# Query and key heads transposed in pairs, with wider gMLP output products and re-spaced spatial products, in a sparse-attention decoder layer

## The chip, the cores and the metric

The kernel runs on one core of a Trainium2 chip. The metric is the time of one execution on the device in microseconds (us). The profile that is read here is that of one further execution of the same program.

## What is computed

One layer of a decoder over a prompt of 2048 positions (16 blocks of 128) and a sample of 64 new positions (8 sequences by 8). All products are of float32 accuracy.

```python
h = rmsnorm(x, norm_g)
z = h @ w_in                       # 1024 -> 3656 columns
q, k, v, qi, ki, wi, ga, u, vm, gm = split(z)
q, k   = rope(rmsnorm(q)), rope(rmsnorm(k))     # 8 query heads, 4 key heads, 64 wide
qi, ki = rope(qi), rope(ki)                     # indexer: 8 heads x 64, one key of 64
score  = sum_h wi[h] * relu(qi[h] @ ki.T)       # causal
mask   = the 256 highest scores of each query
o      = softmax(q @ k.T / 8 over mask) @ v * silu(ga)
vn     = layernorm(gelu(vm))
s      = tril(w_s[group]) @ vn (in chunks of 128 positions) + b_s
gm_out = gelu(u) * s * silu(gm)
r      = x + concat(o, gm_out) @ w_out
y      = r + sigmoid(rmsnorm(r) @ w_ple_gate) * (p @ w_ple_proj)
```

Keys, values, indexer keys and the sample's `vn` are outputs as well. The sample attends to 1024 paged past positions of its own sequence and to the new ones.

## The kernel before

Float32 accuracy comes from splitting an operand into a rounded high part and the remaining low part (`split`, lines 121 to 124: ScalarE copies the high part out of PSUM, VectorE subtracts it for the low part) and adding high by high, high by low and low by high products.

**Phase A** (`phase_a`) goes through the blocks in three rounds (line 55; block 16, called SB, is the sample), and in each round through 14 column chunks of `w_in` (line 57), 256 columns wide except the first, x1, of 328. For each chunk `load_w` brings the weights: in round 0 as eight raw pieces, which GpSimd (line 288) and VectorE (line 289) scale and split, and `keep_w` stores the halves to DRAM; in later rounds the stored halves are loaded. `raw` has six buffers, each weight half two. `proj` makes a chunk's product for a block (24 matmuls), `post` works on it. `spatial` multiplies one of eight groups of `vn` for all blocks of a round at once; it is called while the chunk named k is under way, spread over its blocks.

Beside this, `pump` deals out pieces of the indexer's work after each product: `idx` computes a block's scores (line 683 and 684 for each head and 512 keys; ScalarE takes the relu at line 686, VectorE adds at line 688), `topk` finds the 256th score. A block is primed (its loads are issued) when the one ahead of it starts. The indexer's keys lie in SBUF with the high part in partitions 0 to 63 and the low part in 64 to 127, so a query head has to be present in both halves of the partitions. `load_qi` gets that by loading each head twice side by side, and each of the 8 heads is transposed by itself (line 668).

When the last chunk is done, `gm_product` multiplies the gMLP output by its half of `w_out` (lines 574, 575 and 578), in two halves of 256 columns of a 512-wide result, while the last top-k ends and `prep_early` prepares the attention: `twice` copies each key head next to itself, `prep_kv` transposes 4 heads (line 1016), `prep_q` 8 query heads that were loaded twice (lines 994 and 1031).

**Phase B** (`phase_b`) goes through steps of block and key head: scores (lines 1098 to 1100), exponentials (line 1107), transposed probabilities (line 1133), values (line 1150). The next block's queries are prepared at the third of a block's four steps. **Phase C** does the rest of the output projection, the gate and the result.

The tile framework lays out every engine's order at build time, by a simulation with estimated costs, and waits on semaphores keep the data right. An engine then works through its order as laid out; an instruction whose operand is late holds up all that stand behind it on its engine. DMAs are issued from SP's queue, in order, except gathers, which GpSimd issues.

## Time and profile before

| | |
|---|---|
| median of 3 runs (lowest to highest) | 1905.88 us (1904.62 to 1906.0) |
| profiled execution | 1905.45 us |
| its span, first to last instruction | 1903.7 us |
| TensorE busy in the span | 1845.6 us, 97% |
| VectorE, ScalarE, GpSimd busy | 65%, 54%, 33% |
| mean granted TensorE clock | 0.99 |

PE is TensorE's matmul stream, PEld its weight loads, DVE VectorE, ACT ScalarE, POOL GpSimd, SP the queue that issues most DMAs. Matmuls overlap: one takes longer from start to end than the next one starts behind it, so the distance between starts is what a matmul costs in a dense stream. A busy time counts the union of the spans.

### The profile page before, as it was taken

Reading aid. Unit: us, or ns where it says so; the run is one execution under the profiler, and the core shown is the slowest. Engines: PE = TensorE matmul, PEld = TensorE weight load, DVE = VectorE, ACT = ScalarE, POOL = GpSimd, SP = SyncE. Lnnn points to the kernel's source line nnn. Section 1 sums busy time; section 2 is a strip of 40 time slices with the busy share of each in tenths; the row PEclk is TensorE's granted clock in tenths of the full one; section 3 lists DMA queues with packets and bytes.
Section 4 is the critical chain, followed back from the end, with each engine's and each line's share of the span. In section 5 each row is a group of like instructions: output and inputs, shape, how many; then the busy total and the mean of one; then the engine's idle time right before and its main releaser. Section 6 shows DMA issues by size and latency. Waiting matters only on the chain. (4 is left out here: it accounts for less than half of the span.)

```text
span 1903.7 us, 34773 instructions
## 1 busy us (share of the span) xinstructions
PE 1845.6 (97%) x12374; PEld 1627.9 (86%) x12374; DVE 1244.3 (65%) x3623; ACT 1018.5 (54%) x1909; POOL 629.3 (33%) x950
## 2 busy tenths in 40 slices
PE   7989999999999999999999899999999989999998
PEld 6989979998999999999999777778777767888887
DVE  4597655478778638779852789879898854223321
ACT  4244435246556536676664888768787743222221
POOL 4583463332003224014303543232223164222211
PEclk9989999999999999999999999999999999999999
DMA  8645655644444554454554543232222073222211
GB/s 288 209 157 185 232 177 201 196 130 126 150 149 162 203 181 135 142 184 156 156 183 138 140 115 92 59 109 71 74 59 73 25 252 137 80 96 95 102 36 45
DMA packets 180578, 261.59 MB, mean 137 GB/s; under 512 B 83176, under 2 KB 129968, under 8 KB 176688
## 3 DMA queue, kind: packets, MB, share of 16 engines
q1 hardware_dynamic: 174512, 240.45, 38.8%
q0 software_dynamic: 5888, 18.88, 3.3%
q8 instruction: 98, 1.61, 0.4%
q14 instruction: 80, 0.66, 0.1%
HBM read 171.90 MB, written 87.37 MB: 136 GB/s over the span
## 5 line engine op out<-in xcount | busy, mean ns | idle before, releaser
L319 PE MATMUL z<-whi,hhi 128*128 128x256 f32 (+1 forms) x1792 | 463.2, 292 | 10.7 <-DVE qn L379 2.5
L320 PE MATMUL z<-wlo,hhi 128*128 128x256 f32 (+1 forms) x1792 | 456.9, 288 | 0.2 <-DVE wlo L289 0.2
L319 PEld LDWEIGHTS z<-whi,hhi 128*128 128x128 f32 x1792 | 344.8, 192 | 22.2 <-ACT kin L358 3.2
L320 PEld LDWEIGHTS z<-wlo,hhi 128*128 128x128 f32 x1792 | 345.1, 193 | 5.3 <-DVE wlo L289 1.5
L322 PE MATMUL z<-whi,hlo 128*128 128x256 f32 (+1 forms) x1792 | 270.2, 288 | 0.0
L322 PEld LDWEIGHTS z<-whi,hlo 128*128 128x128 f32 x1792 | 241.8, 192 | 4.0
L688 DVE SCALAR_TENSOR_TENSOR big<-dots,sgn,big 128x1024 f32<-128x1024 f32 (+7 forms) x176 | 179.2, 1018 | 61.0 <-ACT dots L686 59.5
L686 ACT ACTIVATE dots<-dots 128x1024 f32<-128x1024 f32 (+7 forms) x176 | 140.9, 803 | 108.2 <-PE dots L684 104.8
L124 DVE TENSOR_TENSOR b_pt<-b_tp,b_pt 128x512 fp32r<-128x512 f32 (+1 forms) x288 | 183.3, 655 | 11.3 <-ACT b_pt L123 9.8
L1150 PE MATMUL b_o<-b_pt,Vst 128*128 128x512 f32 x544 | 185.0, 425 | 0.6 <-DVE b_pt L124 0.4
L123 ACT ACTIVATE b_pt<-b_tp 128x512 fp32r<-128x512 f32 (+1 forms) x288 | 156.0, 578 | 47.2 <-PE b_tp L1133 37.9
L1133 PE MATMUL b_tp<-mats,b_sm 128*128 128x128 f32 x1088 | 171.8, 276 | 3.8 <-ACT b_sm L1107 2.8
L1107 ACT ACTIVATE b_sm<-b_sm,b_st 128x128 f32<-128x128 f32 (+15 forms) x128 | 154.6, 1209 | 19.5 <-DVE b_st L1100 18.4
L1133 PEld LDWEIGHTS b_tp<-mats,b_sm 128*128 128x128 f32 x1088 | 133.7, 142 | 34.1 <-ACT b_sm L1107 7.3
L824 ACT ACTIVATE bfw<-big,tk 128x384 bf16<-128x384 f32 (+14 forms) x105 | 136.4, 1299 | 48.1 <-DVE tk L844 30.0
L1098 PE MATMUL b_s<-Kst,b_qh 128*128 128x512 f32 (+3 forms) x320 | 140.8, 441 | 7.7 <-DVE b_st L1100 4.5
L1100 DVE CUSTOM_DVE_ANT_0 b_sm<-b_s,b_mask,b_st 128x512 f32<-128x512 f32 (+3 forms) x192 | 123.9, 645 | 27.9 <-PE b_s L1099 23.2
L1099 PE MATMUL b_s<-Kst,b_ql 128*128 128x512 f32 (+3 forms) x320 | 117.4, 369 | 0.0
L683 PE MATMUL dots<-ki_stack,qih 128*128 128x512 f32 (+3 forms) x304 | 113.0, 374 | 1.4 <-DVE big L688 1.4
L684 PE MATMUL dots<-ki_stack,qil 128*128 128x512 f32 (+3 forms) x304 | 110.2, 372 | 0.0
L1150 PEld LDWEIGHTS b_o<-b_pt,Vst 128*128 128x128 f32 x544 | 90.3, 190 | 23.2 <-DVE b_pt L124 6.6
L1460 PE MATMUL c_mm<-c_h_w_ple_gate,c_mh 128*128 128x512 f32 x272 | 109.0, 401 | 0.2 <-ACT c_mh L123 0.2
(350 smaller groups left out, 3871.6 us busy)
## 6 DMA issues: line engine op xcount, KB each, us to landing
whi<-s_wh SPq DMA_DIRECT2D x52, 512.0 KB
wlo<-s_wl SPq DMA_DIRECT2D x52, 512.0 KB
raw<-w_in SPq DMA_DIRECT2D x112, 128.0 KB
s_wh<-whi SPq DMA_DIRECT2D x13, 1024.0 KB
s_wl<-wlo SPq DMA_DIRECT2D x13, 1024.0 KB
s_r<-hlo SPq DMA_DIRECT2D x32, 256.0 KB
b_qr<-s_q SPq DMA_DIRECT2D x32, 256.0 KB
c_r<-s_r SPq DMA_DIRECT2D x16, 512.0 KB
```

The source lines that it names most:

```text
L123: nc.scalar.activation(hi, src, AF.Copy)
L124: nc.vector.tensor_tensor(lo, src, hi.bitcast(F32), OP.subtract)
L319: nc.tensor.matmul(z, lhsT=hh[:, k], rhs=wh[:, k, :n], start=(k == 0), stop=False)
L320: nc.tensor.matmul(z, lhsT=hh[:, k], rhs=wl[:, k, :n], start=False, stop=False)
L322: nc.tensor.matmul(z, lhsT=hl[:, k], rhs=wh[:, k, :n], start=False, stop=(k == 7))
L686: nc.scalar.activation(r, r, AF.Relu)
L688: nc.vector.scalar_tensor_tensor(a, r, self.sgn[:, b, h:h + 1], a, op0=OP.mult, op1=OP.add)
L824: nc.scalar.activation(junk, acc[:P], AF.Sign, bias=cur[:, 0:1], accum_out=cur[:, 1:2])
L1098: nc.tensor.matmul(ps, lhsT=qh[:, h], rhs=rhs, start=True, stop=False)
L1107: nc.scalar.activation(part, part, AF.Exp, bias=stt[:, h, c:c + 1], scale=-1.0, accum_out=stt[:, h, 4 + e:5 + e])
L1133: nc.tensor.transpose(ps[:, k, r], sm2[r][:, (k0 + k) * 128:(k0 + k) * 128 + 128], ident)
L1150: nc.tensor.matmul(o.rearrange("p a b -> p (a b)"), lhsT=Vst[:, kb, g].rearrange("p a d -> p (a d)"), rhs=pt[:, k].rearrange("p a b -> p ( ...
```

## The change

- The two halves of the weights of a chunk are kept with 328 elements from one row of eight to the next in every chunk, not with as many as the chunk is wide. `raw` has four buffers, not six.
- `gm_product` makes one product of 512 columns where it made two of 256; `load_out` places the weights for that.
- The spatial products are spread over the chunks k (from its third block on) and v.
- In round 2 the blocks are scored from 15 down to 11.
- Two heads lie side by side in a load and are transposed together. A new function, `heads`, splits the transposed pair: each head's high and low part are written to the partitions on which it lies, and get to the other half of the partitions by four DMAs within SBUF, or, for attention blocks 0 to 4 (`direct`), by further instructions of ScalarE and VectorE. `idx` does this when a block is primed. `prep_q` is called at a block's first step instead of its third, with the load of the block after. Keys are transposed in pairs as well and written to both halves by ScalarE and VectorE; `twice` goes. The indexer's key is no longer doubled ahead of its transpose, and block SB's is not transposed.
- The iota that seeds a block's scores is made anew for each block on GpSimd (`order`), and the stored one goes. The sample's indexer takes its buffers from the new tiles (not shown).

```diff
-DUE = ROUNDS
+DUE = ROUNDS[:2] + [ROUNDS[2][::-1]]
...
-        rp = pool("a_raw", 6)
+        rp = pool("a_raw", 4)
...
-            return [wp.tile([128, 8 * 328], F32R, name=f"w{e}")[:, :8 * n].rearrange("p (k n) -> p k n", k=8)
-                    for e in ("hi", "lo")]
+            return [wp.tile([128, 8, 328], F32R, name=f"w{e}")[:, :, :n] for e in ("hi", "lo")]
...
-            wh, wl = halves(256)
+            wh, wl = (t.rearrange("p k n -> p (k n)")[:, :2048].rearrange("p (k n) -> p k n", k=4) for t in halves(328))
             for i in range(8):
                 raw = rp.tile([128, 328], F32, name="raw")[:, :256]
-                k, c0 = 4 + i % 4, j * 512 + i // 4 * 256
-                nc.sync.dma_start(raw, I["w_out"][0, k * 128:(k + 1) * 128, c0:c0 + 256])
-                nc.gpsimd.tensor_scalar(wh[:, i], raw, 1.0, 1.0, op0=OP.mult, op1=OP.mult)
-                nc.gpsimd.tensor_tensor(wl[:, i], raw, wh[:, i].bitcast(F32), OP.subtract)
+                k, c0 = i // 2, i % 2 * 256
+                nc.sync.dma_start(raw, I["w_out"][0, 512 + k * 128:640 + k * 128, j * 512 + c0:j * 512 + c0 + 256])
+                nc.gpsimd.tensor_scalar(wh[:, k, c0:c0 + 256], raw, 1.0, 1.0, op0=OP.mult, op1=OP.mult)
+                nc.gpsimd.tensor_tensor(wl[:, k, c0:c0 + 256], raw, wh[:, k, c0:c0 + 256].bitcast(F32), OP.subtract)
...
-                kin2 = wk.tile([128, 2, 64], F32, name="kin")[:P]
-                nc.scalar.activation(kin2, z[:, None, 0:64].to_broadcast([P, 2, 64]), AF.Copy, scale=rs)
-                self.rope(nc.vector, kin2, rt, 2, wk, P)
-                kin = kin2[:, 0]
+                kin = wk.tile([128, 64], F32, name="kin")[:P]
+                nc.scalar.activation(kin, z[:, 0:64], AF.Copy, scale=rs)
+                self.rope(nc.vector, kin[:, None, :], rt, 1, wk, P)
                 dst = O["idx_k_sample"].rearrange("o a t d -> (o a t) d") if b == SB else O["idx_k_prompt"][0, 0, b * 128:(b + 1) * 128]
                 nc.sync.dma_start(dst, kin)
 
                 def ki_t():
                     ps = self.tp.tile([128, 4, 128], F32, name="tp")
-                    nc.tensor.transpose(ps[:, 0, :P], kin2.rearrange("p a d -> p (a d)"), ident[:P, :P])
-                    kst = self.ki[:, b, :P]
-                    nc.scalar.activation(kst, ps[:, 0, :P], AF.Copy)
-                    nc.vector.tensor_tensor(kst[64:128], ps[64:128, 0, :P], kst[64:128].bitcast(F32), OP.subtract)
-
-                later.append(ki_t)
+                    nc.tensor.transpose(ps[:64, 0], kin, ident)
+                    kst = self.ki[:, b]
+                    nc.scalar.activation(kst[0:64], ps[:64, 0], AF.Copy)
+                    nc.vector.tensor_tensor(kst[64:128], ps[:64, 0], kst[0:64].bitcast(F32), OP.subtract)
+
+                if b != SB:
+                    later.append(ki_t)
...
-                iota = ac.tile([128, SEQ], mybir.dt.int16, name="iota")
-                nc.gpsimd.iota(iota, pattern=[[1, SEQ]], base=0, channel_multiplier=0)
-                self.iota = iota
...
-                if name == "k":
-                    for g in range(8 * j // len(blocks), 8 * (j + 1) // len(blocks)):
+                n, s = 2 * len(blocks) - 2, {"k": j - 2, "v": len(blocks) - 2 + j}.get(name, -1)
+                if s >= 0:
+                    for g in range(8 * s // n, 8 * (s + 1) // n):
                         spatial(blocks, g)
...
-            for i in range(2):
-                z = zt[:, i * 256:i * 256 + 256]
+            for k in range(4):
+                nc.tensor.matmul(zt, lhsT=hh[:, k], rhs=wh[:, k], start=(k == 0), stop=False)
+                nc.tensor.matmul(zt, lhsT=hh[:, k], rhs=wl[:, k], start=False, stop=(b == SB and k == 3))
+            if b != SB:
                 for k in range(4):
-                    nc.tensor.matmul(z, lhsT=hh[:, k], rhs=wh[:, i * 4 + k, :256], start=(k == 0), stop=False)
-                    nc.tensor.matmul(z, lhsT=hh[:, k], rhs=wl[:, i * 4 + k, :256], start=False, stop=(b == SB and k == 3))
-                if b != SB:
-                    for k in range(4):
-                        nc.tensor.matmul(z, lhsT=hh[:, 4 + k], rhs=wh[:, i * 4 + k, :256], start=False, stop=(k == 3))
+                    nc.tensor.matmul(zt, lhsT=hh[:, 4 + k], rhs=wh[:, k], start=False, stop=(k == 3))
...
+def order(self, acc, P):
+    nc = self.nc
+    nc.gpsimd.iota(acc[:P], pattern=[[1, acc.shape[1]]], base=0, channel_multiplier=0,
+                   allow_small_or_imprecise_dtypes=True)
+    nc.gpsimd.tensor_scalar(acc[:P], acc[:P], -UNIT, 1.0, op0=OP.mult, op1=OP.mult)
+
+def heads(self, pool, names, ps, bufs, direct=False):
+    nc = self.nc
+    qh, ql = (pool.tile([128, 2, 4, 128], F32R, name=n, bufs=bufs) for n in names)
+    own = [slice(0, 64), slice(64, 128)]
+    for e in range(2):
+        nc.scalar.activation(qh[own[e], e], ps[own[e]], AF.Copy)
+        nc.vector.tensor_tensor(ql[own[e], e], ps[own[e]], qh[own[e], e].bitcast(F32), OP.subtract)
+        if direct:
+            nc.scalar.activation(qh[own[1 - e], e], ps[own[e]], AF.Copy)
+            nc.vector.tensor_tensor(ql[own[1 - e], e], ps[own[e]], qh[own[e], e].bitcast(F32), OP.subtract)
+    if direct:
+        return qh, ql
+    for t in (qh, ql):
+        for e in range(2):
+            nc.sync.dma_start(t[own[1 - e], e].bitcast(F32), t[own[e], e].bitcast(F32))
+    return qh, ql
+
 def idx(self, b):
     nc, wk, wk2 = self.nc, self.wk, self.wk2
     W = 128 * (b + 1)
-    qds = self.load_qi(b)
+    qd = wk2.tile([128, 4, 128], F32, name="qid", bufs=2)
+    nc.sync.dma_start(qd, self.s_qi[b].rearrange("p (h d) -> p h d", h=4))
+    ps = self.tp.tile([128, 4, 128], F32, name="tp")
+    for j in range(4):
+        nc.tensor.transpose(ps[:, j], qd[:, j], self.ident)
+    qh, ql = self.heads(wk2, ("qih", "qil"), ps, 2)
     yield None
-    qh, ql = [], []
-    for j in range(2):
-        qd = qds[j].rearrange("p h a d -> p h (a d)")
-        ps = self.tp.tile([128, 4, 128], F32, name="tp")
-        for h in range(4):
-            nc.tensor.transpose(ps[:, h], qd[:, h], self.ident)
-        qh.append(wk2.tile([128, 4, 128], F32R, name="qih", bufs=3))
-        ql.append(wk2.tile([128, 4, 128], F32R, name="qil", bufs=3))
-        self.split(qh[j], ql[j], ps)
-        yield 2
     acc = self.big.tile([128, SEQ], F32, name="big")[:, :W]
-    nc.gpsimd.tensor_scalar(acc, self.iota[:, :W], -UNIT, 1.0, op0=OP.mult, op1=OP.mult)
+    self.order(acc, 128)
...
-                nc.tensor.matmul(ps[:, s0:s0 + sn], lhsT=qh[h // 4][:, h % 4], rhs=rhs, start=True, stop=False)
-                nc.tensor.matmul(ps[:, s0:s0 + sn], lhsT=ql[h // 4][:, h % 4], rhs=rhs, start=False, stop=True)
+                nc.tensor.matmul(ps[:, s0:s0 + sn], lhsT=qh[:, h % 2, h // 2], rhs=rhs, start=True, stop=False)
+                nc.tensor.matmul(ps[:, s0:s0 + sn], lhsT=ql[:, h % 2, h // 2], rhs=rhs, start=False, stop=True)
...
-        q = io.tile([128, 8, 2, 64], F32, name="b_qr", bufs=1)
+        q = io.tile([128, 4, 128], F32, name="b_qr", bufs=1)
         ga = io.tile([128, 512], F32, name="b_ga")
-        for a in range(2):
-            nc.sync.dma_start(q[:, :, a], self.s_q[i].rearrange("t (h d) -> t h d", h=8))
+        nc.sync.dma_start(q, self.s_q[i].rearrange("t (h d) -> t h d", h=4))
...
-    def twice(i):
-        kds[i] = raw.tile([128, 4, 2, 64], F32, name="b_kd")
-        nc.scalar.copy(kds[i], kvs[i][0].rearrange("p (h d) -> p h d", h=4)[:, :, None, :].to_broadcast([128, 4, 2, 64]))
...
-        k, v = kds.pop(i), kvs.pop(i)[1]
+        k, v = kvs.pop(i)
         ps = psum()
-        for g in range(4):
-            nc.tensor.transpose(ps[:, g], k[:, g].rearrange("p a d -> p (a d)"), ident)
-        ks = Kst[i // 4][:, :, (i % 4) * 128:(i % 4) * 128 + 128]
-        nc.scalar.activation(ks, ps, AF.Copy)
-        V.tensor_tensor(ks[64:128], ps[64:128], ks[64:128].bitcast(F32), OP.subtract)
+        for j in range(2):
+            nc.tensor.transpose(ps[:, j], k[:, j * 128:j * 128 + 128], ident)
+        ks = Kst[i // 4].rearrange("p (j e) n -> p j e n", e=2)[:, :, :, (i % 4) * 128:(i % 4) * 128 + 128]
+        own = [slice(0, 64), slice(64, 128)]
+        for e in range(2):
+            nc.scalar.activation(ks[own[e], :, e], ps[own[e], 0:2], AF.Copy)
+            V.tensor_tensor(ks[own[1 - e], :, e], ps[own[e], 0:2], ks[own[e], :, e].bitcast(F32), OP.subtract)
...
-        qh = qp.tile([128, 8, 128], F32R, name="b_qh")
-        ql = qp.tile([128, 8, 128], F32R, name="b_ql")
-        for j in range(2):
-            ps = psum()
-            for h in range(4):
-                nc.tensor.transpose(ps[:, h], q[:, j * 4 + h].rearrange("p a d -> p (a d)"), ident)
-            self.split(qh[:, j * 4:j * 4 + 4], ql[:, j * 4:j * 4 + 4], ps)
+        ps = psum()
+        for j in range(4):
+            nc.tensor.transpose(ps[:, j], q[:, j], ident)
+        qh, ql = self.heads(qp, ("b_qh", "b_ql"), ps, 2, direct=i < 5)
...
-            if si < len(steps) and g == 2 and at + 1 < NB:
+            if si < len(steps) and g == 0 and at + 1 < NB:
```

## Rows read from the trace of the kernel before

**Rows 1.** The page's first part: busy time, share of the span, instructions.
```profile
span 1903.7 us, 34773 instructions
...
PE 1845.6 (97%) x12374; PEld 1627.9 (86%) x12374; DVE 1244.3 (65%) x3623; ACT 1018.5 (54%) x1909; POOL 629.3 (33%) x950
```
**Rows 2.** Stretches: us, busy PE PEld DVE ACT POOL, granted clock, DMA share, GB/s.
```profile
0.00:50.00 50.00, 38.16 (x195) 33.38 (x196) 25.20 (x78) 19.96 (x48) 25.73 (x61) 0.93 0.85 274
...
500.00:600.00 100.00, 100.00 (x772) 96.83 (x771) 81.75 (x296) 62.80 (x111) 16.39 (x23) 1.00 0.44 146
940.00:1045.00 105.00, 100.53 (x845) 99.32 (x844) 47.63 (x142) 57.49 (x93) 18.58 (x33) 1.00 0.54 177
1045.00:1100.00 55.00, 48.59 (x305) 39.90 (x304) 42.73 (x145) 45.76 (x136) 28.88 (x56) 0.94 0.51 139
1100.00:1500.00 400.00, 395.38 (x2656) 308.52 (x2655) 344.17 (x933) 313.45 (x615) 116.62 (x195) 1.00 0.27 75
```
**Rows 3.** Timeline of TensorE from 507 us: start, duration, instruction, count.
```profile
508.51 0.60 PE L668 MATMUL tp<-mats,qid 128*128 128x128 f32 x4
508.86 0.36 PE L319 MATMUL z<-whi,hhi 128*128 128x256 f32 x1
509.06 0.28 PE L320 MATMUL z<-wlo,hhi 128*128 128x256 f32 x1
509.18 0.29 PE L319 MATMUL z<-whi,hhi 128*128 128x256 f32 x1
```
**Rows 4.** Views of the tiles qid and b_qr: count, shortest/median/longest ns, first and last start.
```profile
L668 PE MATMUL tp<-mats,qid x112: 270/272/328, 69.8 to 823.7; 128*128 128x128 f32 x112
...
L1031 PE MATMUL b_tp<-mats,b_qr x120: 270/272/327, 1052.4 to 1465.8; 128*128 128x128 f32 x120
```
**Rows 5.** Timeline of TensorE from 1050 us.
```profile
1052.40 1.04 PE L1031 MATMUL b_tp<-mats,b_qr 128*128 128x128 f32 x8
```
**Rows 6.** Groups by line: busy us, mean ns, idle before.
```profile
L574 PE MATMUL z<-whi,hhi 128*128 128x256 f32 x272 | 70.1, 290 | 0.0
```
**Rows 7.** Timeline of TensorE from 1650 us.
```profile
1649.95 0.39 PE L1461 MATMUL c_mm<-c_l_w_ple_proj,c_ph 128*128 128x512 f32 x1
...
1650.40 0.39 PE L1461 MATMUL c_mm<-c_l_w_ple_proj,c_ph 128*128 128x512 f32 x1
...
1652.44 0.40 PE L1460 MATMUL c_mm<-c_h_w_out,c_oh 128*128 128x512 f32 x1
...
1652.91 0.40 PE L1460 MATMUL c_mm<-c_h_w_out,c_oh 128*128 128x512 f32 x1
```
**Rows 8.** Timeline of TensorE from 125 us, with idle time before and its releaser.
```profile
129.56 1.43 PE L338 MATMUL tp<-vn,wsT 128*128 128x320 f32 x2 [2.15 <-POOL vn L431]
131.25 0.47 PE L343 MATMUL tp<-vn,wsS 64*64 64x64 f32 x2 [0.26 <-POOL vn L431]
133.53 1.43 PE L338 MATMUL tp<-vn,wsT 128*128 128x320 f32 x2 [1.80 <-ACT vn L339]
```
**Rows 9.** Stretches around that place, columns as in rows 2.
```profile
125.00:129.00 4.00, 1.54 (x9) 0.90 (x8) 4.00 (x11) 1.76 (x5) 4.00 (x4) 0.93 0.97 371
129.00:135.00 6.00, 3.38 (x8) 1.86 (x9) 5.89 (x26) 2.92 (x9) 5.42 (x8) 0.50 0.23 68
```
**Rows 10.** Timelines of SP's queue and of GpSimd at the start.
```profile
2.28 7.64 SPq L282 DMA_DIRECT2D raw<-w_in  x16
...
0.85 1.84 POOL L512 IOTA iota<- 128x2048 int16 x1 [0.40 <-POOLq L1568]
...
6.49 0.54 POOL L288 TENSOR_SCALAR whi<-raw,gk 128x328 fp32r<-128x328 f32 x1 [3.61 <-DMA raw<-w_in]
```
**Rows 11.** View of the tile b_qh: shortest/median/longest ns.
```profile
L123 ACT ACTIVATE b_qh<-b_tp x30: 574/598/712, 1056.0 to 1466.1; 128x512 fp32r<-128x512 f32 x30
L124 DVE TENSOR_TENSOR b_ql<-b_tp,b_qh x30: 672/686/693, 1056.6 to 1467.2; 128x512 fp32r<-128x512 f32 x30
```
**Rows 12.** DMA issues: median us from issue to landing.
```profile
s_pg<-cache_k,prow POOLq DMA_INDIRECT x32, 3.4
```

More of the change, by code (lines that the diff above doesn't have):

```diff
@@ L702, in sample_idx @@
         V = nc.vector
-        qi = wk2.tile([128, 4, 128], F32R, name="qih", bufs=3).bitcast(F32)
+        both = wk2.tile([128, 2, 4, 128], F32R, name="qih", bufs=2).bitcast(F32)
+        qi = both[:, 0]
         nc.gpsimd.memset(qi, 0.0)
@@ L719, in sample_idx @@
         gt = wk2.tile([128, 4, 2, 64], F32, name="qid", bufs=2).rearrange("p h a d -> p (h a d)")[:64]
-        pick = wk2.tile([128, 4, 128], F32R, name="qih", bufs=3)
-        pick = pick.bitcast(F32).rearrange("p a b -> p (a b)")[:64, 0:64].rearrange("p (a b) -> p a b", a=8)
+        pick = both[:64, 1, 0, 0:64].rearrange("p (a b) -> p a b", a=8)
         nc.sync.dma_start(pick, I["c_pick"])
@@ L740, in sample_idx @@
         acc = self.big.tile([128, SEQ], F32, name="big")
+        self.order(acc[:, :WS], 64)
         pgs = {}
@@ L756, in second @@
             nc.tensor.matmul(ds, lhsT=qi[:, p], rhs=kT[:, :n], start=True, stop=True)
-            r = wk2.tile([128, 4, 128], F32R, name="qil", bufs=3).bitcast(F32).rearrange("p a b -> p (a b)")[:, :n]
+            r = wk2.tile([128, 512], F32, name="sr")[:, :n]
             nc.scalar.activation(r, ds, AF.Relu)
@@ L765, in third @@
             if p == 3:
-                V.scalar_tensor_tensor(acc[:64, c * 512:c * 512 + n], self.iota[:64, c * 512:c * 512 + n], -UNIT,
-                                       scs.pop(c)[:64, :n], op0=OP.mult, op1=OP.add)
+                a = acc[:64, c * 512:c * 512 + n]
+                V.tensor_tensor(a, scs.pop(c)[:64, :n], a, OP.add)
         for c in range(3):
@@ L775, in sample_idx @@
                     f()
+                kT = wk2.tile([128, 2, 4, 128], F32R, name="qil", bufs=2).bitcast(F32)[:, 0].rearrange("p a b -> p (a b)")
                 if c < 2:
@@ L781, in sample_idx @@
                         nc.tensor.transpose(ps[:, k], pg[:, k].rearrange("p a d -> p (a d)"), self.ident)
-                    kT = wk2.tile([128, 4, 128], F32R, name="qih", bufs=3).bitcast(F32).rearrange("p a b -> p (a b)")
                     nc.scalar.activation(kT.rearrange("p (x k) -> p x k", k=4), ps.rearrange("p k x -> p x k"), AF.Copy)
@@ L1045, in prep_early @@
         load_q(ORDER[1])
-        twice(0)
         yield
         for i in range(NB):
-            if i + 1 < NB:
-                twice(i + 1)
             prep_kv(i, psum)
@@ L1092, in scores, with chunk @@
                     out.append(sm)
-                    def chunk(c, h=h, sm=sm):
+                    def chunk(c, h=h, sm=sm, r=r):
                         c0, cn = c * 512, min(512, W - c * 512)
@@ L1097, in chunk @@
                         rhs = Kst[c][:, g, :cn]
-                        nc.tensor.matmul(ps, lhsT=qh[:, h], rhs=rhs, start=True, stop=False)
-                        nc.tensor.matmul(ps, lhsT=ql[:, h], rhs=rhs, start=False, stop=True)
+                        nc.tensor.matmul(ps, lhsT=qh[:, r, g], rhs=rhs, start=True, stop=False)
+                        nc.tensor.matmul(ps, lhsT=ql[:, r, g], rhs=rhs, start=False, stop=True)
                         V.tensor_tensor_reduce(out=sm[:, c0:c0 + cn], in0=ps, in1=m[:, c0:c0 + cn], scale=1.0,
```

1 line of the change is left out of this document (removed).

## The prediction

> **What bounds the kernel now.** I read the page's busy time first [rows 1]: TensorE is busy 97% of a span of 1903.7 us, the next engine, VectorE, 65%. An average hides stages, so next the table of stretches [rows 2]. From 500 to 600 us TensorE is busy in every moment and its clock is granted in full, while VectorE works 81.8 of 100 us; from 940 to 1045 it is busy 100.5 of 105. There TensorE alone sets the pace, and what is taken from its stream is taken from the end. Two stretches are different. In the first 50 us it is busy 38.2 and the DMA engines are busy 85% of the time. From 1045 to 1100 us it is busy 48.6 of 55 beside ScalarE with 45.8, and from 1100 to 1500 us 395 of 400 with VectorE at 344 (86%): there a chain of three engines sets the pace, and a saving on TensorE is worth less than its length. The profiled execution took 1905.45 us, 1.75 more than its span, and lies 0.4 below the median of the runs, 1905.88. The bound of "no change" that I use is 0.2%, about 3.8 us.
>
> **Transposes, the largest term.** Four transposes of a query block begin at 508.51, the next product at 508.86, and that one lasts until the next begins at 509.06, 0.20 instead of the 0.12 that the products behind it are apart [rows 3]. So one group of four costs 0.35 + 0.08 = 0.43 us. Eight in a row last 1.04, with one alone lasting 0.27 [rows 4, 5]: (1.04 - 0.27) / 7 = 0.11 each.
> The scores' queries go from 112 transposes (14 blocks by 8) [rows 4] to 56: 14 groups by 0.43 = 6.0 us. The attention's queries go from 128 (120 in phase B [rows 4] and 8 of block 0 before it) to 64: 16 by 0.43 = 6.9 us. The keys go from 64 to 32: 32 by 0.11 = 3.5 us. Together 16.4 us. The key of the indexer keeps its transpose, except block SB's, which goes: nothing.
>
> **The gMLP half of the output projection.** Line 574's group has 272 products [rows 6], line 575 as many and line 578 256: 800 of 256 columns. Products of 256 columns follow each other every 0.12 us [rows 3], so they cost 96 us. They become 400 of 512 columns. In the last stage such products start 0.225 us apart with one weight (1650.40 - 1649.95, two steps) and 0.235 with another (1652.91 - 1652.44) [rows 7]. At 0.23 they cost 92: 4.0 us are saved, 2 to 6 by the two rows. The Trainium skill (TensorE: Matmul & The Clock Gate, section Back-to-back issue gap) gives a warm gap of N / 2.4 + 2.5 ns, which is 109 and 216 ns. By it 800 products would take 87.3 us, 400 would take 86.3, and the saving would be 1.0 us, a sum 3 us later than mine. The rows show a larger fixed part for each product (13 ns at 256 columns), so I stay with them.
>
> **Spatial products spread.** In round 0 the first of them sits in front of TensorE's queue at 129.56 after 2.15 us of idling for the LayerNorm on GpSimd, and the third at 133.53 after 1.80 for ScalarE; 0.26 lie between, from the same view: 4.2 us [rows 8]. From 125 to 129 us TensorE was busy 1.5 of 4, and behind that, from 129 to 135, its granted clock was 0.50, the lower of the two levels, 1.2 GHz [rows 9]. Starting two blocks later gives GpSimd two more blocks' time (24 products by 0.12 = 2.9 us each, 5.8). I take the 4.2. The lower bound is nothing: the order was laid out at build time from estimates, GpSimd was later than estimated, and it can be later again. The upper bound is 9: if the clock stays up, 16 products at 0.21 instead of 0.12 and the groups beside them cost some 5 us less.
>
> **What costs nothing.** The reversed order of the last scores: it moves the top-k's end, but from 940 to 1045, where that falls, TensorE has no idle time to give [rows 2]. GpSimd writes an iota for each block, at most 1.84 us [rows 10], about 20 us in all beside 16.4 us of work in 100; if GpSimd were late, VectorE's additions would be, then the two score buffers and TensorE. The 16 copies of keys that ScalarE loses are off the path (57.5 us of 105). The weights 328 apart change no row's product that I can find, so I take nothing; they cut the DMA's pieces from 4 and 8 KB to 1 KB, covered by a DMA share of 0.44 to 0.54 later on [rows 2] but not at the start.
>
> **Costs.** *Start.* Of the weights' first eight pieces six may be in flight now, four after. GpSimd gets the first 4.2 us after the queue began to issue (2.28 to 6.49), and waits for later ones too [rows 10]. The fifth piece must wait until the first has been split, about 7.6, instead of being issued near 6.2. That is 1.5 us later, and the transfers of x queue behind it on SP. I take 2 us (0 to 4, the upper end one landing).
> *Direct splits, blocks 0 to 4.* Each half costs a full instruction, 0.60 us on ScalarE and 0.69 on VectorE [rows 11]; there are four and four instead of two and two. For the four blocks inside phase B that is 4 by 2 by 0.60 = 4.8 us on ScalarE and 5.5 on VectorE, in the stretch from 1045 on where ScalarE is busy 83%. Behind them wait the exponentials and the split of the probabilities, and behind those TensorE. Bounds 0 and 5.5; I take 2.5, because the steps there also have idle moments on all engines.
> *Phase B's coupling.* 11 blocks by 0.43 = 4.7 us of the saved query transposes fall where VectorE is at 86%. I take half back: 2.4 (0 to 4.7).
> *Halves by DMA.* For 14 scored blocks and 11 attention blocks, four transfers from SBUF to SBUF now stand between the split and the first product. No row shows such a transfer. The nearest are a gather's 3.4 us [rows 12] and the 4.2 us of the start. Preparing moves with all its parts (load, transposes, splits, four DMAs) one scored block or two steps ahead, past the mask's load on SP, and the product that waits has every later product behind it on TensorE. A scored block lasts far longer than 4 us, except that the first block of each of the three rounds is used at once. I take 2 us.
>
> **The sum.** Gains 16.4 + 4.0 + 4.2 = 24.6; costs 2 + 2.5 + 2.4 + 2 = 8.9; net 15.7. From 1905.45 that is 1889.8, and with the 0.4 to the median 1890. With each bound taken badly, all the query savings of phase A's end and B lost (16.4 - 6.9 = 9.5), 2, 0 and costs of 4 + 5.5 + 2, nothing is left: 1906. With each taken well (16.4 + 6 + 9, no cost) it is 1874.
>
> **Rivals.** *The stall and the low clock go altogether, and phase B follows TensorE.* For it: rows 9, a low clock right behind the stall. Against it: GpSimd gets extra work. 9 instead of 4.2, and 2.4 and 2.5 not paid: some 10 us more, 1880.
> *The chains keep phase B and the start costs more.* For it: ScalarE and VectorE at 83 and 86% [rows 2]. Phase B gives nothing (4.5 less), the start 4 instead of 2, the spatial wait half: 8 to 9 less, 1898.
> *Nothing in the net*: the bad bounds above, 1906.
> *Slower: the halves land late.* The first product of a scored block waits for its DMA, and TensorE's queue with it. Each such wait costs 3.4 to 4.2 us, 3.8 say. Without this term the sum saves 17.7, so five exposed blocks eat it; if all 14 scored blocks wait, 53 us are lost and the time is 1941. For it: queries now need two transfers in a row, and SP's queue, in order, is shared with the weights. Against it: the old loads of the queries, one block ahead too, made TensorE wait nowhere that I found. The Trainium skill (DMA: Bandwidth & Descriptors, section Anatomy of one DMA) puts a fixed cost of about 2.0 us on a DMA whatever its size; by that 14 waits would be 28 us and the time 1916. No row here shows it for such a copy.
> *The change does not do what it says* has a place in the reversed order alone, and there it costs nothing either way.
>
> **Chances.** Forecast 0.42 (its own range 1884 to 1896), 1880 case 0.18, 1898 case 0.15, nothing 0.11, late halves 0.14. Faster by over 0.2% are the first three: 0.75; the same 0.11; slower 0.14. The range leaves out the late halves and a little beyond the good bounds: 1874 to 1910.
>
> **What would show it.** Right: 152 transposes fewer, at about 0.11 apart in each group; products of line 574's successor every 0.23 us; no idle time of over 1 us before a spatial product and no clock of 0.50 behind 125 us; phase B shorter by 2 to 5 us. Wrong: idle time of TensorE ended by a DMA that writes a half of the queries, in phase A above all; or a start, up to the second chunk, more than 4 us later; or ScalarE near 100% in the first blocks of phase B.

## The result and the profile after

The changed kernel takes 1937.37 us (median of 4 runs, 1935.98 to 1945.24) beside 1905.25 for the kernel before in the same session: 1.0173 times as long, interval 1.016 to 1.0187, some 33 us slower. The prediction was 1890 us, and its range ended at 1910. The profiled execution is the longest of the four, 1945.24 us.

The page's first part of the changed kernel, for [rows 1]:
```profile
span 1943.5 us, 33818 instructions
...
PE 1836.2 (94%) x11821; PEld 1597.0 (82%) x11821; DVE 1249.2 (64%) x3648; ACT 1021.2 (53%) x1918; POOL 642.1 (33%) x965
```
TensorE works 9 us less, as it should with fewer transposes, and the span is 40 us longer: what was saved was not on the path. Its stretches, columns as in [rows 2]:
```profile
0.00:50.00 50.00, 35.86 (x192) 32.49 (x193) 24.60 (x79) 20.10 (x50) 20.67 (x57) 0.90 0.81 246
...
135.00:150.00 15.00, 11.27 (x62) 10.14 (x63) 11.46 (x57) 6.69 (x18) 9.56 (x14) 0.77 0.50 155
...
500.00:600.00 100.00, 96.83 (x715) 92.36 (x714) 77.34 (x276) 61.20 (x105) 17.55 (x23) 0.97 0.46 148
...
1000.00:1030.00 30.00, 12.63 (x51) 9.74 (x50) 18.20 (x72) 13.29 (x23) 4.90 (x10) 0.66 0.35 112
1030.00:1082.00 52.00, 44.67 (x204) 34.86 (x203) 16.21 (x35) 20.93 (x47) 13.10 (x23) 0.93 0.37 121
1082.00:1137.00 55.00, 46.11 (x265) 35.31 (x263) 43.91 (x145) 47.43 (x140) 28.55 (x55) 0.91 0.37 113
1137.00:1537.00 400.00, 391.79 (x2612) 304.74 (x2606) 345.18 (x935) 314.29 (x615) 116.63 (x195) 1.00 0.29 83
```
The new hole is at 1000 to 1030 us: TensorE is busy 12.6 of 30 us and its granted clock is 0.66, between its two levels, where the kernel before was busy 100.5 of 105 us at the full clock. The timeline of TensorE there, with the products 512 wide ahead of it:
```profile
999.65 0.39 PE L569 MATMUL z<-whi,hhi 128*128 128x512 f32 x1
999.88 0.40 PE L570 MATMUL z<-wlo,hhi 128*128 128x512 f32 x1
...
1005.82 1.07 PE L573 MATMUL z<-whi,hhi 128*128 128x512 f32 x4
1023.58 0.66 PE L1023 MATMUL tp<-mats,b_kr 128*128 128x128 f32 x2 [16.69 <-issue]
```
It idles 16.7 us in front of the transposes of a key block. These need one of two PSUM tiles (`tp`), and the two key blocks ahead of them, transposed at 989 and 1001 us, hold both until they are split. ScalarE and VectorE, in the same stretch:
```profile
1013.79 0.63 ACT L1027 ACTIVATE Kst<-tp 64x256 fp32r<-64x256 f32 x2
...
1016.76 1.76 DVE L874 MAX8 v<-big 128x8 f32<-128x1536 f32 x1
...
1022.19 1.63 DVE L1028 TENSOR_TENSOR Kst<-tp,Kst 64x256 fp32r<-64x256 f32 x4
```
ScalarE's half of the first split is done ahead of the last MAX8. VectorE's half (L1028) stands behind the last top-k in VectorE's order, comes 8.4 us later and frees the tiles. So the question is when the top-k ends. The view of the line of MAX8, one of the last steps of each block's search, behind which a score buffer comes free, over the third round (count, shortest/median/longest ns, first and last start), first before and then after:
```profile
L860 DVE MAX8 v<-big x5: 1754/2016/2281, 776.4 to 984.1; 128x8 f32<-128x1536 f32 x1, 128x8 f32<-128x1664 f32 x1, 128x8 f32<-128x1792 f32 x1, 128x8 f32<-128x1920 f32 x1
```
```profile
L874 DVE MAX8 v<-big x5: 1761/2018/2281, 808.4 to 1016.8; 128x8 f32<-128x2048 f32 x1, 128x8 f32<-128x1920 f32 x1, 128x8 f32<-128x1792 f32 x1, 128x8 f32<-128x1664 f32 x1
```
The last one is 32.7 us later, and the first product of phase B follows it by 64.0 us before (1048.1) and 64.9 after (1081.7). That is most of the loss: of the 39.8 us between the two profiled executions 32.7 are there by then, and 0.9 come in front of phase B, 3.5 in it and 2.7 in phase C. I call the time between the round's first and last MAX8 its chain, the time from round 1's last MAX8 to it the first link, and that from the last MAX8 to phase B the tail. The changed kernel has 139.8 us in the first link, the kernel before 120.4; the chain is 208 in both; 13 us were lost earlier.

The same stages of all kernels run (us, each from its own profiled execution; phase B is counted from its first product to the first of phase C). The change against the kernel before is that of the timed runs, (ratio - 1) x 1905:

| kernel | change, us (interval of the ratio) | first link | chain | last MAX8 | tail | B | C |
|---|---|---|---|---|---|---|---|
| before | 0 | 120.4 | 207.7 | 984.1 | 64.0 | 494.5 | 361.1 |
| after | +33.0 (1.016 to 1.0187) | 139.8 | 208.3 | 1016.8 | 64.9 | 498.0 | 363.8 |
| e1 | +21.5 (1.0096 to 1.0129) | 120.3 | 218.3 | 1002.1 | 62.9 | 497.1 | 357.5 |
| e2 | +3.6 (1.0004 to 1.0035) | 129.7 | 201.9 | 990.1 | 69.1 | 493.0 | 358.3 |
| e3 | +8.4 (1.0031 to 1.0056) | 120.4 | 208.7 | 989.8 | 65.0 | 498.5 | 358.8 |
| e4 | +10.9 (1.0038 to 1.0077) | 120.4 | 209.1 | 986.2 | 62.8 | 496.4 | 367.3 |
| e5 | +5.3 (1.0017 to 1.0039) | 109.0 | 216.2 | 991.3 | 62.1 | 494.9 | 359.1 |
| e6 | +2.9 (1.0004 to 1.0025) | 117.5 | 216.6 | 996.3 | 62.5 | 492.3 | 359.2 |
| e7 | -3.6 (0.9971 to 0.999) | 120.4 | 208.4 | 981.1 | 63.8 | 494.5 | 361.3 |
| e8 | -5.7 (0.9957 to 0.9982) | 116.9 | 210.3 | 985.9 | 64.4 | 494.6 | 357.3 |
| e9 | +24.0 (1.0105 to 1.0146) | 133.6 | 212.0 | 1009.8 | 61.5 | 494.1 | 360.4 |
| e10 | -11.8 (0.9921 to 0.9955) | 116.9 | 207.8 | 977.5 | 63.7 | 494.6 | 357.5 |
| e11 | -9.0 (0.9936 to 0.997) | 116.9 | 208.1 | 977.3 | 63.9 | 494.7 | 357.5 |
| e12 | +1.1 (0.9996 to 1.0015) | 120.4 | 208.1 | 985.3 | 63.3 | 499.1 | 356.8 |
| e13 | +23.8 (1.0108 to 1.0142) | 117.6 | 223.4 | 1005.2 | 60.1 | 497.6 | 361.6 |
| e14 | +3.4 (1.0008 to 1.0029) | 119.8 | 209.4 | 982.2 | 68.9 | 492.6 | 362.5 |
| e15 | -1.3 (0.9983 to 1.0002) | 116.8 | 216.6 | 992.5 | 63.3 | 490.5 | 357.3 |
| e16 | +22.1 (1.0099 to 1.0133) | 120.4 | 208.9 | 987.1 | 64.5 | 509.0 | 366.3 |
| e17 | +5.0 (1.0013 to 1.0038) | 123.1 | 216.7 | 992.7 | 65.9 | 494.0 | 357.3 |
| e18 | +2.7 (1.0002 to 1.0025) | 116.9 | 209.6 | 978.4 | 63.9 | 497.7 | 367.2 |

While the last MAX8 moves over 39 us, the tail stays between 60 and 69. The end of the top-k sets the end of the first phase. The tail's length doesn't go with TensorE's work. The tail of the kernel before and that of the changed one, columns as in [rows 2]:
```profile
984.10:1048.10 64.00, 59.53 (x500) 58.32 (x499) 22.34 (x48) 28.86 (x54) 18.02 (x32) 1.00 0.46 153
```
```profile
1016.80:1081.70 64.90, 50.11 (x218) 39.00 (x219) 24.34 (x64) 22.69 (x52) 17.99 (x32) 0.85 0.34 112
```
TensorE is busy 9.4 us less, at a lower granted clock, and the tail is as long. What paces its 16 key blocks stays open.

### The profile page after: what moved, and what is told of

The parts are those of the page before. It is cut to its first block, busy times and chain, and to the rows that moved or that the text cites. A ratio compares the mean times of both kernels' runs of the same rounds, so it can differ in the third digit from the quotient of the medians.

```text
span 1943.5 us, 33818 instructions
## 1 busy us (share of the span) xinstructions
PE 1836.2 (94%) x11821; PEld 1597.0 (82%) x11821; DVE 1249.2 (64%) x3648; ACT 1021.2 (53%) x1918; POOL 642.1 (33%) x965
## 5 line engine op out<-in xcount | busy, mean ns | idle before, releaser
L318 PE MATMUL z<-whi,hhi 128*128 128x256 f32 (+1 forms) x1792 | 465.2, 293 | 20.3 <-DVE qn L378 11.5
L321 PE MATMUL z<-whi,hlo 128*128 128x256 f32 (+1 forms) x1792 | 264.9, 287 | 0.0
```

The source lines that it names most:

```text
L318: nc.tensor.matmul(z, lhsT=hh[:, k], rhs=wh[:, k, :n], start=(k == 0), stop=False)
L321: nc.tensor.matmul(z, lhsT=hl[:, k], rhs=wh[:, k, :n], start=False, stop=(k == 7))
```

## Experiments

**e1: the changed kernel with the old order; e2: the kernel before with the new one.**
```diff
-DUE = ROUNDS[:2] + [ROUNDS[2][::-1]]
+DUE = ROUNDS
```
e2 has the same line the other way round in the kernel before.

> The changed kernel with one edit undone: the last five score blocks come in the order 11 to 15 again. Theory 1 (the reversed order): the chain of top-k evaluations sets the end of the first phase, and with the widest block first it starts one wide block of products later (first MAX8 of the round 140 us after the one before it in the changed kernel, 120 us in the kernel before); TensorE runs out of other work behind it. Then most of the loss comes back: 1892 to 1910 us, the last MAX8 near 985 to 1000 us instead of 1016.8, no 16.7 us TensorE gap near 1020 us. Theory 2 (the other parts: half copies of queries by DMA, direct splits between the top-k evaluations, four raw buffers): the order is neutral, 1925 to 1940 us, and the gap in front of the keys of the second phase stays.

> The kernel before with the reversed order of the last five score blocks and nothing else. Theory 1: 1920 to 1940 us, with the last products of the scores 30 to 45 us later than 938.6 and a TensorE gap ahead of the second phase. Theory 2: 1903 to 1908 us, no measurable change.

The order is worth 11.5 us in the changed kernel (33.0 - 21.5) and 3.6 by itself. Neither theory holds as a whole. e1's 1925.4 us lies at the edge of theory 2's range, and the hole stays (20.4 us at 1009.7), so most of the loss is elsewhere; but the order isn't neutral. e2's 1910.0 lies between the two ranges. In e1 the first link is back at 120.3 us, but the chain is 218.3. In e2 the first link grows by 9.3, the chain, now without the widest block and with the narrowest, shrinks by 5.8, and the tail grows by 5.1.

**e3, e12, e16: the second phase's edits in the kernel before.** e3 takes the new `prep_kv`, `prep_q`, `heads`, the two `qh[:, r, g]` products and `g == 0`; e12 the new `prep_kv` alone; e16 is e3 with
```diff
-            qh, ql = self.heads(qp, ("b_qh", "b_ql"), ps, 2, direct=i < 5)
+            qh, ql = self.heads(qp, ("b_qh", "b_ql"), ps, 2)
```

> The kernel before with the second-phase edits alone: keys and queries transposed in pairs, direct splits in blocks 0 to 4, DMA halves behind them, query preparation at g 0. By the terms of the prediction: 16 x 0.43 = 6.9 and 32 x 0.11 = 3.5 us of transposes less 2.5 of direct splits and 2.4 of coupling, so 1898 to 1902 us. Theory 2: the direct splits, issued between the last top-k evaluations, and the four partition-half instructions for each key block cost more than the transposes give: 1908 to 1920 us.

> The kernel before with the keys of the second phase alone transposed in pairs (64 fewer 128-column copies on ScalarE and 32 fewer transposes, two ScalarE and two VectorE instructions for one each). The prediction's term is 3.5 us less: 1901 to 1904 us. If the loss of the second-phase edits (1912.8 with keys and queries) is the keys' (four short instructions for each of 16 blocks behind the top-k's end): 1908 to 1912 us; if it is the queries', 1903 to 1906 us here.

> The second-phase edits alone (1912.8 us) with the queries of blocks 0 to 4 too made by DMA halves instead of direct splits. Keys alone are neutral (1905.95), so some 7 us are the queries'. Theory E (the direct splits hold ScalarE and VectorE in the first blocks, which they bound): 1904 to 1908 us. Rival F (in blocks this short the DMA halves come too late: the prediction's fourth rival): 1914 to 1922 us.

The keys cost nothing in the time, though phase B itself is 4.6 us longer; the queries cost 7.3 (8.4 - 1.1). Where, stays open: phase B is as long in e3 as in e12, and of the 7.7 us between their profiled executions 3.9 are there at the start of the third round (651.2 and 647.3), ahead of all that these edits touch. Theory E, which blames the direct splits, falls: with copies in their place the time is 13.7 more, and phase B 10.5 longer. What the direct splits cost beside the old form isn't shown. Who waited for whom in phase B of e16 (total, times, longest, us):
```profile
PE b_s L1104 <- DMA b_qh<-b_qh: 6.9, 3, 4.4
...
PE b_s L1105 <- DMA b_ql<-b_ql: 2.3, 2, 1.4
```
The early blocks are too short for a copy to hide in, so the direct split is the cheaper of the two there.

**e4, e11: the products 512 wide.** `load_out` and `gm_product` as in the change, in the kernel before (e4) and in e10 below (e11).

> The kernel before with the output weights as four tiles of 512 and the 34 products of the last stage 512 columns wide instead of two 256-wide halves, all else as before (six raw buffers, the other weights packed). The prediction's term is 4.0 us (2 to 6): 1899 to 1904 us. If TensorE has slack in that stage because the top-k sets its end: 1904 to 1907 us.

> The same with the 512-wide products of the last stage added. If the 10 us that they cost alone belong to the edit (idle TensorE behind the top-k, where they save nothing): 1904 to 1908 us. If these 10 us came from the order in which the third phase's first instructions were laid out, which the edit moved by chance (first products of that phase only 2.8 us late, its end 8.9 us): another layout here, 1894 to 1900 us.

Alone it lost 10.9 us, more than either range allows, of which the table has 6.2 in phase C, where nothing was edited. On e10 that loss is absent: 2.8 us by the ratios, whose intervals overlap, and the spans are equal (1893.3 and 1893.5). The stretch from the last MAX8 to phase B, in e10 and then in e11:
```profile
977.00:1041.00 64.00, 59.83 (x502) 58.61 (x502) 22.86 (x48) 28.93 (x54) 18.01 (x32) 1.00 0.48 156
```
```profile
977.00:1041.00 64.00, 58.15 (x282) 46.88 (x281) 22.70 (x48) 27.87 (x52) 18.01 (x32) 0.95 0.42 139
```
TensorE is busy 1.7 us less in the wider form, and the tail is as long as it was.

**e5, e9: no copies of halves for the scores' queries.** e5 is e1, e9 the changed kernel, each with
```diff
-        qh, ql = self.heads(wk2, ("qih", "qil"), ps, 2)
+        qh, ql = self.heads(wk2, ("qih", "qil"), ps, 2, direct=True)
```

> The changed kernel with the old order of the last five blocks, and the queries of the scores split onto both partition halves by ScalarE and VectorE, with no DMA of halves (so also in blocks 5 to 15). Theory 1 (the top-k chain is the pace, and the DMA halves start it late in each round): the 2 us and 1.2 us TensorE waits for the half copies at 390 and 696 us go, the first MAX8 of rounds 1 and 2 comes 4 to 7 us earlier than in the run with the old order alone (454.0 and 783.8 us), and 1912 to 1920 us. Rival (the extra four instructions on ScalarE and VectorE, which carry the chain, cost as much): 1922 to 1932 us.

> The changed kernel with one edit undone: the queries of the scores are split directly, without the DMA halves; the last blocks stay reversed. It completes a square with the changed kernel (1937), the old order with DMA halves (1925) and the old order without (1911). Theory 1a (the two add up, each moves the start of the chain by itself): reversal costs 12 and the halves 14 to 16, so 1921 to 1925 us. Theory 1b (they act on one another: the widest block's query tile is both the last written and the one waited for through a second DMA): the reversal alone costs 3 to 5 as in the kernel before, so 1912 to 1917 us.

The copies cost 16.2 us with the old order (21.5 - 5.3) and 9.0 with the new (33.0 - 24.0). Without them the order costs 18.7, so theory 1b falls, and the two don't simply add either (1929.0 us, where theory 1a had 1921 to 1925). For e5, theory 1 had the time nearly right (1911.2 us), but only one of its two signs: the first MAX8 of the third round comes 8.7 us earlier (775.1 beside 783.8), that of the second round doesn't (455.5 beside 454.0). Where the copies act is seen at the start of the third round. TensorE and SP's queue in e1:
```profile
686.12 1.04 PE L683 MATMUL tp<-mats,qid 128*128 128x128 f32 x8
696.30 0.50 PE L696 MATMUL dots<-ki_stack,qih 128*128 128x512 f32 x1 [1.20 <-DMA qih<-qih]
```
```profile
688.33 0.58 SPq L673 DMA_DIRECT2D qih<-qih  x1
...
694.65 1.51 SPq L673 DMA_DIRECT2D qil<-qil  x2
```
and TensorE in e5:
```profile
682.30 1.04 PE L683 MATMUL tp<-mats,qid 128*128 128x128 f32 x8
687.32 0.39 PE L696 MATMUL dots<-ki_stack,qih 128*128 128x512 f32 x1
```
With copies 10.2 us pass from the transposes to the first product, without them 5.0 (in the kernel before 3.5: 684.53 to 688.03). TensorE idles only 1.2 of the 10.2, since other projections fill it; the top-k behind the products gets the delay. Of the 8.7 us at the round's first MAX8, 2.7 are there when the round starts (647.5 and 644.8).

The product waits for the first copy alone. It is issued at 688.33, and its semaphore is complete at 696.25. The Trainium skill (DMA: Bandwidth & Descriptors, section Issuing engines are not separate DMA queues) calls the time to initiate a DMA usually small relative to the DMA itself; the trace agrees, with 0.58 us of the first copy's 7.9. What the copy met is a full set of DMA engines, 98% busy, with the round's weights and the queries themselves ahead of it. The stretch in e1, columns as in [rows 2], and two of SP's own waits between the eight copies (total, times, longest us):
```profile
683.00:697.00 14.00, 12.80 (x106) 12.39 (x105) 3.00 (x5) 3.65 (x7) 1.11 (x4) 1.00 0.98 279
```
```profile
SPq L673 <- DMA whi<-s_wh: 1.4, 2, 1.0
SPq L673 <- DMA qid<-s_qi: 1.1, 2, 0.6
```
In the kernel before the share is 0.68 from 681 to 695 us. That the weights now come in smaller pieces isn't the reason: e6 below keeps them as they were, has 0.98 too, and 9.6 us pass there from the transposes to the product. In the changed kernel the second round shows the same (copy issued at 381.78, product at 390.84); in its third, where block 15 comes first, only 5.9 us pass.

**e6, e15: the scores' query edits in the kernel before** (`heads`, `idx`, `sample_idx`, `order` of the change, four raw buffers); e15 puts back what the pump charged:
```diff
         yield None
+        yield 2
+        yield 2
```

> The kernel before with the score-query edits alone: pairs transposed, halves by DMA, the four units that a block's preparation was charged left out, the positions made by GpSimd in every block, and four raw buffers, which they need for their memory. By the prediction's terms: 14 x 0.43 = 6.0 less 2 for the halves and 2 for the four buffers, so 1902 us. Theory 1 (each round's chain starts with the halves' latency, and the last top-k ends later by as much): last MAX8 10 to 18 us later than 984.1, 1912 to 1922 us.

> The score-query edits alone (1910.9 us, against 1902.5 for the four raw buffers that they share) with the two charged steps of two units per block put back. Theory C (without these steps the pump hands out products and top-k steps of one block in another alternation, and the round's chain of 216.6 us from first to last MAX8 is 9 us longer for it): 207 to 210 us again, 1900 to 1904 us. Rival D (the 9 us are the halves and the split in four instructions for each block): no change, 1908 to 1913 us.

e6's last MAX8 is 12.2 us later, as theory 1 had it, with the longer chain, 216.6 us; beside e7, which has the four buffers alone, it costs 6.5. e15 is faster by some 4 us, but its chain is 216.6 too, so theory C falls as the reason for it. What these units gain lies elsewhere: the second round's first MAX8 comes at 448.2 instead of 453.7, the third round starts at 643.7 instead of 646.9 and phase B takes 1.8 less. That first MAX8 is at 443.9 in e7, so the score-query edits delay it by 9.8 us. It is late in e5 too, without copies (455.5), and not in e17 below (441.4), so neither the copies nor the positions alone explain it. Which step does stays open.

**e7, e8, e10: what paid.** e7 is the kernel before with `pool("a_raw", 4)`, e8 with the change's lines around `spatial`, e10 with both.

> The kernel before with four raw weight buffers in place of six and nothing else. The prediction's term is 2 us later (0 to 4): 1905 to 1909 us, all of it before the second chunk of weights. Rival: the start hides it and the later chunks, whose weights come back whole, need no raw tiles: 1904 to 1906 us.

> The kernel before with the spatial products spread over the chunks k and v alone. The prediction's term is 4.2 us less (0 to 9), from the stalls near 130 us and the low clock behind them: 1896 to 1905 us. Rival (the stalls are in front of the top-k chain, which resets at each round, so what is won there is lost at the next round's start, or the plan of the engines moves): 1903 to 1912 us.

> The kernel before with the two edits that paid by themselves: four raw buffers and the spread spatial products. If they add (-3.6 and -5.7 us): 1895 to 1898 us. If both took the same start-of-round slack: 1899 to 1903 us.

-3.6, -5.7 and together -11.8 us, more than the sum: e10, 1893.49 us beside 1905.06, is faster than both kernels. e7 is below both of its ranges: the second chunk's first product comes at 46.8 us instead of 49.1 (45.3 to 49.5 in all kernels with four buffers, 49.1 to 50.9 in all with six), and the table's stages behind the second round hardly differ. The prediction's reason for the spread isn't seen: e8 still waits 2.15 us at 131.8 for GpSimd and 1.81 at 135.8 for ScalarE, as in [rows 8]. e8's profiled execution, the slowest of its six, is only 1.5 us below that of the kernel before: its third round's first link is 3.5 shorter, but its last MAX8 1.8 later, and phase C, which has no edit in it, 3.8 shorter. So most of what can be seen of its gain is in a phase that it doesn't touch.

**e13, e14: block 11 first, the others reversed,** in the changed kernel and in e10:
```diff
+DUE = ROUNDS[:2] + [[11, 15, 14, 13, 12]]
```

> The changed kernel with the last round's order 11, 15, 14, 13, 12: the block whose queries are projected first comes first, the rest stays reversed. Theory A (the reversed order costs because block 15's queries are the last that chunk x2 writes and, loaded as one tile of eight heads, its products wait for all of them): the transposes of the round's first queries come at 685 to 690 us instead of 706.4, its first MAX8 some 118 to 122 us after the one before instead of 139.8, the shorter last top-k stays, 1912 to 1922 us. Rival B (descending widths themselves cost, because a wide top-k is behind while narrow products wait for memory): little comes back, 1928 to 1937 us.

> The kernel before with four raw buffers and the spread spatial products (1893.5 us) and the order 11, 15, 14, 13, 12 in the last round. Theory A: the start of the round's chain is as with ascending order, and its last link is one of 13 columns blocks instead of 16, as in the reversed order alone (first to last MAX8 201.9 us against 207.7): 1887 to 1893 us. Rival B: 1895 to 1903 us.

The first transposes of the round come at 686.8 us in e13 instead of 706.0, and the first link is 117.6 instead of 139.8: the start of theory A holds. Block 15's queries are the last that the second chunk writes, and the new `idx` loads all eight heads as one tile. But the chain then takes 223.4 us, and only 9.2 of 33.0 us come back, which is near rival B's range. On e10 this order costs 15.2: last MAX8 4.7 later, tail and phase C 5 each. A reversed order doesn't pay in any form tried; why the chain is longer in e13 stays open.

**e17, e18: one edit each on e10.** e17 drops the stored positions:
```diff
-        nc.gpsimd.tensor_scalar(acc, self.iota[:, :W], -UNIT, 1.0, op0=OP.mult, op1=OP.mult)
+        self.order(acc, 128)
```
e18 takes `prep_kv` as e12 does.

> The fastest kernel so far (four raw buffers and spread spatial products, 1893.5 us) with one more of the change's edits: no stored positions, GpSimd makes them anew in each block (an iota, then a multiplication). Theory G (a block whose products wait for an accumulator's memory gets it behind two GpSimd instructions with other work between them, not one: first accumulation 8 to 11 us behind the MAX8 that frees it, not 5.3): the last round's chain of 207.8 us grows to 213 to 218 us, and 1898 to 1905 us. Rival H (GpSimd has idle time, which the prediction counted it as: no cost; the 9 us are the splits in four): 206 to 209 us, 1891 to 1895 us.

> The same fastest kernel with the second phase's keys transposed in pairs, the one other edit that cost nothing alone (1905.95 us beside 1905.06). If its 32 transposes come off TensorE's path behind the top-k: 1889 to 1892 us. If the tail behind the last MAX8 is paced by the keys' chain through ScalarE and VectorE whatever their transposes take (62 to 65 us in nearly all kernels): 1892 to 1896 us.

e17 costs 16.8 us, and its chain is 216.7 against 207.8, as theory G had it. GpSimd behind the MAX8 that frees the memory for block 15, in e10 (that MAX8 starts at 881.3) and in e17 (at 890.9):
```profile
883.44 1.90 POOL L675 TENSOR_SCALAR big<-iota 128x2048 f32<-128x2048 int16 x1 [0.88 <-DVE v L861]
```
```profile
892.99 1.84 POOL L658 IOTA big<- 128x2048 f32 x1 [2.47 <-DVE v L865]
894.91 0.62 POOL L811 TENSOR_TENSOR tk<-tk,half 128x1 f32<-128x1 f32 x1
895.62 2.82 POOL L660 TENSOR_SCALAR big<-big 128x2048 f32<-128x2048 f32 x1
```
The accumulator is ready 4.0 us behind the MAX8 in e10 and 7.5 in e17, since a second instruction and another block's work stand in GpSimd's order. VectorE's first addition follows at 886.70 (5.4) and 898.57 (7.7). Three of the round's blocks wait for memory in this way, 9.9 us more over the three, though GpSimd is busy only 33% of the changed kernel's span. The time, 1912.1 us, is above theory G's range, since the first link is 6.2 longer too and the tail 2.2.

e18 costs 14.5 more than e10, which neither expectation had, 9.7 of it in phase C. TensorE there:
```profile
1575.71 0.51 PE L1455 MATMUL c_mm<-c_l_w_ple_gate,c_mh 128*128 128x512 f32 x1 [2.89 <-DVE c_l_w_ple_gate L1408]
...
1580.14 1.11 PE L1438 MATMUL c_tp<-mats,c_rn 128*128 128x128 f32 x4 [3.09 <-DVE c_pl L124]
```
The stretches around that place, in e18 and, about as far from phase C's start, in e10:
```profile
1570.00:1590.00 20.00, 14.01 (x62) 10.91 (x61) 16.77 (x12) 5.43 (x10) 15.37 (x10) 0.83 0.46 151
```
```profile
1565.00:1585.00 20.00, 18.36 (x88) 14.87 (x88) 16.64 (x13) 7.80 (x12) 13.62 (x9) 1.00 0.37 130
```
TensorE meets a weight that VectorE hasn't split yet and idles 6.0 us of the stretch, where it idles 1.6 in e10; the granted clock is 0.83 there and 1.00 in e10. No line of that phase differs between the two kernels; the order in which its first instructions were laid out does. That this order is the whole reason isn't shown.

## Why the prediction was wrong, by its steps

**What bounds the kernel: wrong, and everything else hangs on it.** I read 100.5 busy us of 105 as "TensorE alone sets the pace", so that "what is taken from its stream is taken from the end" [rows 2]. TensorE was filled with products that were waiting to be done, while the stage's end was set by the top-k and the 60 to 69 us behind it. e11 and the changed kernel's tail show it from one side (less TensorE work, as long a tail), the table from the other: 32.7 of the 39.8 us are the last MAX8's. Of the three signs of being wrong that the prediction names, the first came as a single wait of 1.8 us for a half, the others not: the second chunk starts at 49.5 us beside 49.1, and ScalarE is busy 47.4 of phase B's first 55 us. The end of the top-k wasn't among them.

**Transposes, 16.4 us: the count right, the worth wrong.** The views of the tiles in the changed kernel, for [rows 4]:
```profile
L683 PE MATMUL tp<-mats,qid x56: 270/272/327, 78.5 to 797.1; 128*128 128x128 f32 x56
...
L1037 PE MATMUL b_tp<-mats,b_qr x60: 270/272/422, 997.8 to 1473.6; 128*128 128x128 f32 x60
...
L1023 PE MATMUL tp<-mats,b_kr x32: 270/272/448, 989.4 to 1078.0; 128*128 128x128 f32 x32
```
No run that takes some of them out is faster for it: e12 +1.1 us, e3 +8.4, e6, with the copies and the positions, 6.5 above e7.

**Products 512 wide, 4.0 us: the distance right, the worth not.** 999.65 to 999.88 is the predicted 0.23; no gain on e10.

**Spatial products, 4.2 us: sign and size right (5.7 alone), by luck, since the mechanism is wrong.** e8 keeps both waits. In the changed kernel TensorE waits 3.4 us for GpSimd at 137.2, and the granted clock of the stretch behind is 0.77, not 1.00.

**What costs nothing: here two of the largest errors stand.** The reversed order "moves the top-k's end, but ... TensorE has no idle time to give": the top-k's end was the thing to price, and 11.5 to 18.7 us are its price among the other edits. GpSimd's iota was priced by GpSimd's idle time, with the right chain behind it ("VectorE's additions would be, then the two score buffers") and no price: 16.8 us in e17.

**Halves by DMA, 2 us: mis-sized, 9 to 16.** Also the rival had the wrong mechanism: it charged TensorE's waits at 3.8 us each, and over the first phase the changed kernel shows one, of 1.8 us. The delay goes into the chain of top-k steps instead. A copy's price was too low as well: the prediction took 3.4 and 4.2 us from other transfers, and the one followed in e1 took 7.9 with the DMA engines 98% busy. That its 1941 lies near 1937 is no proof of it.

**Phase B: no gain where 6.9 + 3.5 less 2.5 and 2.4 were expected.** Keys gave nothing (e12; 14.5 lost on e10, in e18) and queries cost 7.3 (e3 less e12), and phase B became longer by 3.5 us, not shorter by 2 to 5. ScalarE is busy 47.4 of its first 55 us, not near 100%, and the direct splits are the better of the two ways (e16); whether their 2.5 us were right isn't shown, and which step of the queries costs isn't settled.

**Start, 2 us for four buffers: wrong in sign.** e7 is 3.6 us faster, and its second chunk begins 2.3 us earlier, not later. Why fewer buffers are faster wasn't tried.

The single prices don't add up: iota 16.8, queries 7.3, products 2.8, less 11.8, make 15.1, where e5, which has these edits, the smaller ones and the saved transposes, lost 5.3. Part of the difference is phase C, which varies from 356.8 to 367.3 us without an edit in it. So each price holds for its base: e6 has the iota too and costs only 6.5 in all. The weights kept 328 apart and the indexer's key that is no longer doubled weren't run by themselves.

## What to carry to other kernels

An engine that is busy 95% of a stage may only be filled; what sets the stage's end is found by asking what its successor waits for, and whether that moves in step with it. Price an edit to a small engine or a DMA by the delay it puts into the longest serial chain, however idle the engine is, and look for it at the places where that chain waits for memory; for a DMA, look at what is under way when it is issued. Where the order of instructions is laid out from estimates, an edit can move the time of a stage that it doesn't touch, so try it on two bases before giving it a price.

## What the runs showed that I had not expected

- The kernel before and e2 run the same instructions in the same order on TensorE, VectorE, ScalarE and GpSimd up to 396 us, but the first product of the scores starts at 73.5 us in one and at 76.9 in the other: single executions differ by over 3 us at the start.
- A copy of 128 KB within SBUF, issued in 0.58 us at a round's start, took 7.9 us until its semaphore was complete, with the DMA engines 98% busy.
- A 16.7 us hole in TensorE's work came with a granted clock of 0.66 over 1000 to 1030 us.
